# Memory keys and values projected in 512 columns per bank, keys of all four heads normed together

## The chip, the cores and the metric

The kernel runs on one core of one Trainium2 chip. The metric is device time in microseconds (us) for one execution. The five engines are named as in the profile: PE is TensorE's products (PEld its weight loads), DVE is VectorE, ACT is ScalarE, POOL is GpSimd, and SP issues most of the DMAs. Each engine takes its instructions strictly in the order in which the program holds them.

## The reference

One layer of a decoder trunk over 1024 tokens of width 1024. The input `x` is normed and projected; three branches (a sparse attention, a convolution module, and cross-attention into 256 memory tokens) are gated, merged, projected and added to `x`; a feed-forward part follows. The change concerns the keys and values of the cross-attention:

```python
kvm = rms_norm(mem, norm_mem) @ w_mem_kv          # mem (256, 1024), w_mem_kv (1024, 2 * 512)
km, vm = jnp.split(kvm, 2, axis=-1)
km = rms_norm(km.reshape(b, -1, MEM_HEADS, MEM_HEAD_DIM), mem_qk_norm[1])   # 4 heads of 128
vm = vm.reshape(b, -1, MEM_HEADS, MEM_HEAD_DIM)
s_m = jnp.einsum('bshd,bmhd->bhsm', qm, km) * (MEM_HEAD_DIM ** -0.5)
o_m = jnp.einsum('bhsm,bmhd->bshd', jax.nn.softmax(s_m), vm)
gm = jax.nn.sigmoid(g_merge)                      # three merge gates, 3 * 1024 columns of w_in
```

## The kernel before, in words

Every product of two float32 matrices is made of three passes: both operands are split into a rounded part and a remainder, and `mm3` adds high x high, high x low and low x high in one PSUM bank. A split is a cast on ScalarE (`split`, L131) and a subtraction, mostly on VectorE (L132). Weights come in units of 512 KB through a staging tile (`st`, two buffers) and are split into a buffer of 128 x 2 x 1024.

Weight buffers lie in two pools: `wsp` with three (tiles `wsl`) and `wfp` with two (tiles `fsl`). A pool gives its buffers out in the order in which the program asks, so a later tile waits until the tile that held its buffer has been read for the last time. The helper `anyslab` takes from both: its own counter `turn[0]` sends calls 2 and 4 of every five to `wfp`. PSUM has seven banks for general use (`ps`) and one (`pf`) for the merge gates while these run.

The stages in order of time: the rows of `x` are normed (`norm_row`) and turned into XN (`turn_pair`, whose two parts are L227 on ScalarE and L228 on VectorE), with the memory queries' projection (`queries`) between them; the convolution's inputs, whose 124 taps (L466, L467) run on VectorE along the later projections; the branch gates (L489 to L507, weights `wg`); the compression of the block keys and values (`compress`, weights `cmp_w1`); the memory rows, normed and turned into MN; the memory keys KM and values VM; the memory attention, along with the sparse attention's query projection; that attention's keys and values; the sparse attention itself; then the three output projections with the gates, the output product, and the feed-forward part.

Before the change, keys and values are made in four rounds of two weight units each. A round (`tok_proj` over `row_units`) covers 256 columns, two heads, for both token tiles, and puts them side by side in one bank; each product has 256 columns. The keys of two heads are normed (`heads_norm`), scaled (`gain_mul`), transposed and split before the next round begins.

The order on each engine is made by a scheduler. It takes instructions by a priority, which is their place in the program unless the code changes it, and by its own estimate of when each can start. The merge-gate products (L1016 to L1034) are written under `low(FILL)`, which puts them behind everything else: they are taken where the scheduler sees TensorE free. There are 24 of these weight units, each used for two halves of 24 products, 48 groups in all; the first twelve units may run at any time, the others are tied to points spread over the sparse attention. Each unit has a buffer of `wfp`, and each group the single bank `pf`, emptied by ScalarE (L1033). In the texts below these products are called fillers.

Of the kernel before, what the change touches and what calls it, by code (L numbers as in the profile page):

```python
# [17 lines left out]
P = 128  # L18
# [3 lines left out]
KT = D // P  # L22
# [17 lines left out]
def hybrid_layer_kernel(  # L40
# [4 lines left out]
    nc = tc.nc  # L45
    x, mem, out = x[0], mem[0], out[0]
    w_in, w_mem_kv, w_out = w_in[0], w_mem_kv[0], w_out[0]
# [19 lines left out]
    def nm(s):  # L67
        count[0] += 1
        return f"{s}_{count[0]}"
# [16 lines left out]
    def t4(shape, dt=F32):  # L86
        return t4p.tile([P] + shape, dt, tag="t4", name=nm("t4"))

    def t2(shape, dt=F32, p=P):
        return t2p.tile([p] + shape, dt, tag="t2", name=nm("t2"))  # L90
# [8 lines left out]
    def bank(shape, dt=F32, p=P, at=None):  # L99
        if at is None:  # L100
            turn[1] += 1
            at = order[turn[1] % len(order)]
        return psp[at].tile([p] + shape, dt, tag=f"ps{at}", name=nm("ps"))
# [26 lines left out]
    def split(hi, lo, src, eng=None):  # L130
        m = nc.scalar.copy(hi, src)  # L131
        return m, (eng or nc.vector).tensor_tensor(lo, src, hi.bitcast(F32), op=OP.subtract)  # L132
# [12 lines left out]
    def mm(o, a, b, start, stop):  # L145
        m = nc.tensor.matmul(o, a, b, start=start, stop=stop)  # L146
        n = 1
        for d in o.shape[1:]:
            n *= d
        products.append((m.ins, n if a.dtype == F32R else 4 * n))  # L150
        return m

    def mm3(o, ah, al, bh, bl, start, stop):
        first = mm(o, ah, bh, start, False)
        mm(o, ah, bl, False, False)
        mm(o, al, bh, False, stop)
        return first
# [8 lines left out]
    ident = identr.bitcast(F32)  # L166
# [115 lines left out]
    def row_units(w, c0, alloc=wslab, eng=None):  # L282
        return [unit(w[u * 512:(u + 1) * 512, c0:c0 + 256].rearrange("(k p) c -> p k c", p=P), [4, 256], alloc, eng)
                for u in range(2)]
# [7 lines left out]
    def tok_proj(ws, tp, act=xn, alloc=bank, between=None):  # L292
        o = alloc([2, 256])
        for tt in range(2):
            if tt == 1 and between is not None:
                between()
            t = 2 * tp + tt
            half, a = t // 4, (t % 4) * P
            for k in range(KT):
                w = ws[k // 4]  # L300
                mm3(o[:, tt, :], act(0, k, half, a, a + P), act(1, k, half, a, a + P), w[:, 0, k % 4, :],
                    w[:, 1, k % 4, :], k == 0, k == KT - 1)
        return o

    def wide_unit(w, c0, u, alloc=wslab):

        st = stage.tile([P, 2, 512], F32, tag="st", name=nm("st"))
        nc.sync.dma_start(st, wide_rows(w, c0, u))
        if alloc is t4:
            w_ = (t4([2, 512], F32R), t4([2, 512], F32R))  # L310
        else:
            w_ = alloc([2, 2, 512])
            w_ = (w_[:, 0], w_[:, 1])
        split(w_[0], w_[1], st)
        return w_

    def wide_rows(w, c0, u):
        return w[u * 256:(u + 1) * 256, c0:c0 + 512].rearrange("(k p) c -> p k c", p=P)
# [76 lines left out]
    b = bank([2 * KT])  # L395
    nc.tensor.transpose(b, rows, ident[:2 * KT, :2 * KT])
    nc.vector.tensor_copy(gcol, b)
    ws = [wide_unit(w_in, C_QM, u, alloc=slab) for u in range(2)]
# [31 lines left out]
    b = bank([4, TAPS + 3])  # L430
# [5 lines left out]
    b = bank([2, 16])  # L436
# [58 lines left out]
    for half in range(2):  # L495
        c = slice(half * 512, (half + 1) * 512)
        ps = bank([512])
# [6 lines left out]
    b = bank([NT, 24])  # L504
# [78 lines left out]
    def mn(hl, k, half, a, b):  # L583
        return MN[k // 4][:, hl, k % 4, a:b]

    KM = slab([2, 4, 256])
    VM = slab([2, 2, 512])
    for hp in range(2):
        ps = tok_proj(row_units(w_mem_kv, hp * 256), 0, mn).rearrange("p t (h d) -> p t h d", h=2)
        if hp == 0:  # L590
            turn_keys(cat, products[-1][0])
            compress_out(1, hv, products[-1][0])
        kn = t2([2, 2, P])
        heads_norm(ps, kn)
        gain_mul(kn, gm[:, 1, :])
        b = bank([2, 256])
        for h in range(2):
            for tt in range(2):
                nc.tensor.transpose(b[:, h, tt * P:(tt + 1) * P], kn[:, tt, h, :], ident)
        split(KM[:, 0, 2 * hp:2 * hp + 2, :], KM[:, 1, 2 * hp:2 * hp + 2, :], b)  # L600
    for hp in range(2):
        ps = tok_proj(row_units(w_mem_kv, 512 + hp * 256), 0, mn)
        split(VM[:, 0, :, hp * 256:(hp + 1) * 256], VM[:, 1, :, hp * 256:(hp + 1) * 256], ps)

    msc, exps, stored = float(P) ** -0.5, [], []

# [100 lines left out]
    ws = [wide_unit(w_in, C_Q, u, alloc=slab if u == 3 else wslab) for u in range(4)]  # L707
# [13 lines left out]
    ws = [wide_unit(w_in, C_KV, u, alloc=t4 if u == 3 else wslab) for u in range(4)]  # L721
# [9 lines left out]
    for t in range(NT):  # L731
# [5 lines left out]
        kn = t2([2, 2, 64])  # L737
# [278 lines left out]
    with low(FILL):  # L1016
        j, ws = 0, {}
        halves = [(n_, h_) for n_ in range(3 * KT) for h_ in range(2)]
        halves[-4:] = [(n_, h_) for h_ in range(2) for n_ in (3 * KT - 2, 3 * KT - 1)]
        for n_, h_ in halves:  # L1020
# [5 lines left out]
            ps = fbank([512])  # L1026
# [72 lines left out]
    for n_, (br, wt) in enumerate(branches):  # L1099
        ins = nxt  # L1100
        for dp in range(4):
            w = unit(wt[0, :, dp * 256:(dp + 1) * 256].rearrange("(k p) c -> p k c", p=P), [4, 256],
                     alloc=anyslab if n_ else fslab if dp < 2 else wslab,
# [5 lines left out]
            for d_ in (2 * dp, 2 * dp + 1):  # L1109
# [6 lines left out]
                for half in range(2):  # L1116
                    z = zz[:, half * 512:(half + 1) * 512]
                    ps = (anybank if n_ or dp < 2 and half else bank)([512])
# [5 lines left out]
                    a = acc[dp][:, d_ % 2, half * 512:(half + 1) * 512]  # L1124
# [454 lines left out]
```

## Time and profile before

| what | value |
|---|---|
| median of 3 runs | 1663.55 us (1663.47 to 1663.68) |
| profiled execution, first to last instruction | 1663.0 us; the profile gives no other time of its own, and the median lies 0.5 us above |
| TensorE busy | 1630.5 us |
| VectorE, ScalarE, GpSimd busy | 1103.2, 746.5, 669.7 us |
| mean granted clock of TensorE | 0.998 |
| memory keys and values | 216 to 260 us of the span |
| memory attention and sparse attention's projections | up to about 428 us |
| sparse attention | about 428 to 830 us |

Busy time is an average over stages with different limits, and a matmul counts as busy until its modelled end, so that short waits between products do not show as idle. What a wait is worth is read in its own stage: from the timeline, which shows the instructions of an engine in order of time with the idle time before each in brackets and what ended it, and from the busy times by stage.

### The profile page before, as it was taken

The page shows a single profiled execution, that of the slowest core. Times are in us where ns is not written, and L with a number is a line of the kernel's source. Part 1 is how long each engine was busy: PE and PEld are TensorE (multiplying, and loading weights), DVE is VectorE, ACT ScalarE, POOL GpSimd, SP SyncE. Part 2 cuts the span into 40 slices and gives each one's busy share as a digit, 9 for nine tenths or more (in the row PEclk, how much of TensorE's full clock was granted, in tenths as well). Part 3 has the DMA queues.
Part 4 walks back from the last instruction along what each step waited for, and adds up shares of the span by engine and source line. Part 5 has one row for each costly group of instructions (what it writes and reads, how often), then busy time and mean ns, then how long its engine had stood idle before and what let it go on. Part 6 is the DMA issues. An engine that isn't in the chain of part 4 may idle for free.

```text
span 1663.0 us, 22705 instructions
## 1 busy us (share of the span) xinstructions
PE 1630.5 (98%) x7952; PEld 1363.2 (82%) x7952; DVE 1103.2 (66%) x1829; ACT 746.5 (45%) x1371; POOL 669.7 (40%) x564
## 2 busy tenths in 40 slices
PE   7999999999999999999999999999999999999999
PEld 6888898777878888888788888788888888888887
DVE  6489989798666666557586867865445555376655
ACT  6311354442577666666665355533222232243332
POOL 0011003572467767555215431565657767400000
PEclk9999999999999999999999999999999999999999
DMA  8453456664355556447754442233333445893763
GB/s 283 157 182 102 152 152 178 203 192 125 108 143 167 165 163 177 134 133 249 245 193 140 177 126 115 89 116 100 97 125 123 153 156 183 297 391 108 241 216 126
DMA packets 252218, 277.89 MB, mean 167 GB/s; under 512 B 24308, under 2 KB 174116, under 8 KB 250566
## 3 DMA queue, kind: packets, MB, share of 16 engines
q1 hardware_dynamic: 245190, 263.83, 49.3%
q10 hardware_dynamic: 6912, 12.59, 2.0%
q8 instruction: 63, 1.03, 0.3%
q14 instruction: 53, 0.43, 0.1%
HBM read 191.43 MB, written 84.93 MB: 166 GB/s over the span
## 4 chain that ended last, share of the span: by engine, by line
PE 71%; DVE 4%; POOL 2%; issue 2%; ACT 2%; DMA 1%; SPq 0%; DVEq 0%; POOLq 0%; ACTq 0%
PE ps L146 37%; PE pf L146 15%; PE ps L1513 11%; PE ps L1287 4%; PE ps L965 2%; PE pf L1513 1%; DVE slab L467 1%; POOL slab L666 1%; PE pf L1287 1%; POOL t L643 0%; ACT t L637 0%; DMA wd<-wsl 0%; POOL t L132 0%; PE ps L951 0%; DVE t L132 0%
## 5 line engine op out<-in xcount | busy, mean ns | idle before, releaser
L146 PE MATMUL ps<-slab,wsl 128*128 128x512 f32 (+2 forms) x1688 | 362.8, 373 | 0.3 <-ACT slab L131 0.3
L146 PEld LDWEIGHTS ps<-slab,wsl 128*128 128x128 f32 x1688 | 298.2, 188 | 57.4 <-issue 1.2
L146 PE MATMUL pf<-slab,fsl 128*128 128x512 f32 x1236 | 309.5, 394 | 3.6 <-ACT fz L1033 3.3
L146 PEld LDWEIGHTS pf<-slab,fsl 128*128 128x128 f32 x1236 | 226.9, 188 | 49.0 <-ACT fz L1033 5.7
L1409 DVE TENSOR_TENSOR t<-ps,t 128x512 f32<-128x512 f32 x130 | 89.0, 689 | 120.6 <-PE ps L146 119.3
L467 DVE SCALAR_TENSOR_TENSOR slab<-slab,cw 128x1019 f32<-128x1019 f32 (+16 forms) x120 | 166.0, 1387 | 1.4
L146 PE MATMUL ps<-slab,fsl 128*128 128x512 f32 x684 | 164.4, 394 | 2.0 <-DVE slab L132 1.2
L146 PE MATMUL ps<-slab,slab 128*128 128x512 f32 (+1 forms) x628 | 155.1, 381 | 6.9 <-POOL slab L666 4.1
L146 PEld LDWEIGHTS ps<-slab,fsl 128*128 128x128 f32 x684 | 128.7, 189 | 30.4 <-DVE slab L132 1.6
L146 PEld LDWEIGHTS ps<-slab,slab 128*128 128x128 f32 x628 | 113.7, 190 | 31.7 <-POOL slab L666 5.9
L1513 PE MATMUL ps<-wsl 128*128 128x512 f32 x495 | 118.9, 389 | 0.0
L1513 PEld LDWEIGHTS ps<-wsl 128*128 128x128 f32 x495 | 92.9, 188 | 19.3
L132 DVE TENSOR_TENSOR wsl<-st,wsl 128x1024 fp32r<-128x1024 f32 x58 | 83.7, 1445 | 32.6 <-ACT wsl L131 31.7
L131 ACT CAST wsl<-st 128x1024 fp32r<-128x1024 f32 x61 | 64.0, 1050 | 75.7 <-PE ps L146 30.3
L146 PE MATMUL ps<-wsl,slab 128*128 128x512 f32 (+1 forms) x480 | 97.2, 349 | 0.4 <-DVE slab L228 0.3
L146 PE MATMUL ps<-slab,qt 128*128 128x384 f32 (+6 forms) x400 | 93.8, 338 | 0.8 <-DVE sm L841 0.7
L146 PE MATMUL ps<-t,slab 128*128 128x256 f32 (+1 forms) x404 | 88.5, 319 | 1.5 <-DVE t L132 1.1
L146 PEld LDWEIGHTS ps<-wsl,slab 128*128 128x128 f32 x480 | 76.4, 189 | 11.3 <-DVE slab L228 0.5
L1422 POOL TENSOR_TENSOR t<-t,t 128x512 f32<-128x512 f32 x21 | 39.9, 1900 | 112.7 <-DVE t L1409 55.5
L131 ACT CAST wsl<-t 128x1024 fp32r<-128x1024 f32 x43 | 45.3, 1054 | 87.6 <-POOL t L128 28.7
L1513 PE MATMUL ps<-fsl 128*128 128x512 f32 x330 | 80.2, 389 | 0.0
L1130 POOL TENSOR_TENSOR slab<-slab,t 128x512 f32<-128x512 f32 x32 | 47.8, 1515 | 80.3 <-DVE t L1129 80.3
(255 smaller groups left out, 2942.5 us busy)
## 6 DMA issues: line engine op xcount, KB each, us to landing
t<-in_w_down_dram SPq DMA_DIRECT2D x70, 256.0 KB, 3.9
fst<-in_w_in_dram SPq DMA_DIRECT2D x24, 512.0 KB, 4.2
zd<-fz ACTq DMA_DIRECT2D x48, 256.0 KB, 2.4
slab<-wd SPq DMA_DIRECT2D x24, 512.0 KB, 4.6
t<-zd SPq DMA_DIRECT2D x24, 512.0 KB, 3.4
st<-in_w_gate_dram SPq DMA_DIRECT2D x22, 512.0 KB, 3.8
st<-in_w_up_dram SPq DMA_DIRECT2D x22, 512.0 KB, 4.2
ad<-t SPq DMA_DIRECT2D x44, 256.0 KB, 2.3
```

The costliest lines, as they stand in the source:

```text
L131: m = nc.scalar.copy(hi, src)
L132: return m, (eng or nc.vector).tensor_tensor(lo, src, hi.bitcast(F32), op=OP.subtract)
L146: m = nc.tensor.matmul(o, a, b, start=start, stop=stop)
L467: return nc.vector.scalar_tensor_tensor(acc[:, s:], u[:, :S - s], cw[:, ct, 30 - s:31 - s], acc[:, s:], op0=OP.mult, op1=OP.add)
L666: part = nc.gpsimd.tensor_tensor(PT[:, 1, mb], PT[:, 1, mb].bitcast(F32), PT[:, 0, mb].bitcast(F32), op=OP.subtract)
L965: nc.tensor.transpose(b[:, j - j0, h, :], tiles[h][:, j * P:(j + 1) * P], ident)
L1130: nc.gpsimd.tensor_tensor(a, a, z, op=OP.add)
L1287: nc.tensor.matmul(B[j], a_(ha, k, j), w[:, hb, k % 2, :], start=start and k == 0 and n_ == 0, stop=stop and k == 3 and n_ == 2, skip_grou ...
L1409: nc.vector.tensor_tensor(o, a_, b_, op=OP.add)
L1422: nc.gpsimd.tensor_tensor(u4, u4, c22, op=OP.mult)
L1513: nc.tensor.matmul(B[t], a_, b_, start=start and k == 0 and j == 0, stop=k == FH - 1 and j == 2, skip_group_check=True)
```

## The change

The four rounds become two halves. Each half loads four weight units of 256 rows by 512 columns (`wide_unit` instead of `row_units`, with `anyslab` as the allocator), and makes for each of the two token tiles one bank of 512 columns, with products of 512 columns. The keys of a token tile, all four heads, are normed and scaled at once; they are kept, and transposed and split between the value products.

```diff
-    for hp in range(2):
-        ps = tok_proj(row_units(w_mem_kv, hp * 256), 0, mn).rearrange("p t (h d) -> p t h d", h=2)
-        if hp == 0:
+    def mem_proj(ws, tt):
+        o = bank([512])
+        for k in range(KT):
+            hi, lo = ws[k // 2]
+            mm3(o, mn(0, k, 0, tt * P, tt * P + P), mn(1, k, 0, tt * P, tt * P + P), hi[:, k % 2, :], lo[:, k % 2, :],
+                k == 0, k == KT - 1)
+        return o
+
+    ws = [wide_unit(w_mem_kv, 0, u, alloc=anyslab) for u in range(4)]
+    kns = []
+    for tt in range(2):
+        ps = mem_proj(ws, tt).rearrange("p (a h d) -> p a h d", a=1, h=4)
+        if tt == 0:
             turn_keys(cat, products[-1][0])
             compress_out(1, hv, products[-1][0])
-        kn = t2([2, 2, P])
+        kn = t2([1, 4, P])
         heads_norm(ps, kn)
         gain_mul(kn, gm[:, 1, :])
-        b = bank([2, 256])
-        for h in range(2):
-            for tt in range(2):
-                nc.tensor.transpose(b[:, h, tt * P:(tt + 1) * P], kn[:, tt, h, :], ident)
-        split(KM[:, 0, 2 * hp:2 * hp + 2, :], KM[:, 1, 2 * hp:2 * hp + 2, :], b)
-    for hp in range(2):
-        ps = tok_proj(row_units(w_mem_kv, 512 + hp * 256), 0, mn)
-        split(VM[:, 0, :, hp * 256:(hp + 1) * 256], VM[:, 1, :, hp * 256:(hp + 1) * 256], ps)
+        kns.append(kn)
+    ws = [wide_unit(w_mem_kv, 512, u, alloc=anyslab) for u in range(4)]
+    for tt in range(2):
+        ps = mem_proj(ws, tt)
+        b = bank([4, P])
+        for h in range(4):
+            nc.tensor.transpose(b[:, h, :], kns[tt][:, 0, h, :], ident)
+        c = slice(tt * P, (tt + 1) * P)
+        split(KM[:, 0, :, c], KM[:, 1, :, c], b)
+        split(VM[:, 0, tt, :], VM[:, 1, tt, :], ps)
```

Before, all eight units took `wsl` buffers. Now `anyslab` gives five of them `wsl` and three `fsl`, ahead of the fillers' units in the program. Its counter stands eight calls further at every later use (the second and third branch's weights, the last products of the feed-forward part), so that there the two pools alternate from another point on.

The order on the engines changes well before the edited lines. In the following rows, which the engine takes from top to bottom, `ps` and `pf` are PSUM banks, the first name behind the arrow is the streamed operand and the second the stationary one; a number behind the tile tells one tile from the next. First TensorE, between the convolution's last products (`ps_1201`) and the branch gates' (`ps_1252`, whose stationary operand is `wg`). Before:

```order
L146 MATMUL ps_1201<-slab_406,wsl_1117 128x512 x6
L146 MATMUL pf_6652<-slab_403,fsl_6621 128x512 x6
L146 MATMUL pf_6652<-slab_404,fsl_6621 128x512 x6
L146 MATMUL pf_6652<-slab_405,fsl_6621 128x512 x6
L146 MATMUL pf_6652<-slab_406,fsl_6621 128x512 x6
L146 MATMUL ps_1252<-slab_196,t_170_1247 56x512 x4
```

Now:

```order
L146 MATMUL ps_1201<-slab_404,wsl_1117 128x512 x6
L146 MATMUL ps_1201<-slab_405,wsl_1117 128x512 x6
L146 MATMUL ps_1201<-slab_406,wsl_1117 128x512 x6
L146 MATMUL ps_1252<-slab_196,t_170_1247 56x512 x4
L146 MATMUL ps_1252<-slab_197,t_170_1247 56x512 x4
```

The 24 fillers between the two are gone. In the same way the first 24 fillers have left the projections of `x`, and 24 more the compression.

Second, TensorE at the memory keys: `slab_1556` and `slab_1557` are MN, `ps_1606` before and `ps_1616` now the first keys. Before:

```order
L146 MATMUL pf_6685<-slab_198,fsl_6682 128x512 x4
L146 MATMUL pf_6685<-slab_199,fsl_6682 128x512 x6
L146 MATMUL ps_1606<-wsl_1598,slab_1556 128x256 x11
L146 MATMUL pf_6713<-slab_403,fsl_6682 128x512 x6
L146 MATMUL pf_6713<-slab_404,fsl_6682 128x512 x6
L146 MATMUL pf_6713<-slab_405,fsl_6682 128x512 x6
L146 MATMUL pf_6713<-slab_406,fsl_6682 128x512 x2
L146 MATMUL ps_1606<-wsl_1598,slab_1556 128x256
L146 MATMUL ps_1606<-wsl_1603,slab_1557 128x256 x12
```

Now, with the first value products (`ps_1720`) among them:

```order
L236 MATMUL ps_1585<-identr,slab_1481 128x128 x3
L146 MATMUL ps_1616<-wsl_1598,slab_1556 128x512 x6
L146 MATMUL ps_1616<-fsl_1603,slab_1556 128x512 x6
L146 MATMUL ps_1616<-wsl_1608,slab_1557 128x512 x5
L146 MATMUL ps_1720<-wsl_1702,slab_1556 128x512 x6
L146 MATMUL ps_1616<-wsl_1608,slab_1557 128x512
L146 MATMUL ps_1616<-fsl_1613,slab_1557 128x512 x6
```

No filler stands here any more, and the weights come from both pools. The first filler of the new order (`pf_6528`) stands behind 84 of the 96 memory products.

Third, ScalarE just ahead of the memory keys, where L227 makes the parts of MN. Before:

```order
L131 CAST wsl_1687<-st_1685 128x1024
L552 ACTIVATE t_207_1544,sm_1545<-ps_1541 128x64
L227 ACTIVATE slab_1556<-ps_1558,gcol 128x256
L227 ACTIVATE slab_1556<-ps_1567,gcol 128x256
L138 ACT_TABLE_LOAD
L138 ACTIVATE sm_1547<-sm_1545 128x1
L227 ACTIVATE slab_1557<-ps_1576,gcol 128x256
```

Now:

```order
L552 ACTIVATE t_207_1544,sm_1545<-ps_1541 128x64
L138 ACT_TABLE_LOAD
L138 ACTIVATE sm_1547<-sm_1545 128x1
L227 ACTIVATE slab_1556<-ps_1558,gcol 128x256
L131 CAST wsl_1702<-st_1700 128x1024
L227 ACTIVATE slab_1556<-ps_1567,gcol 128x256
L227 ACTIVATE slab_1557<-ps_1576,gcol 128x256
```

The table load has moved ahead of all eight parts, and the cast of a value weight (`wsl_1702`) between the first and the second of them.

## The prediction

> **What bounds the kernel now.** I read the page's busy shares and chain first, then the stages. The page:
>
> ```profile
> PE 1630.5 (98%) x7952; PEld 1363.2 (82%) x7952; DVE 1103.2 (66%) x1829; ACT 746.5 (45%) x1371; POOL 669.7 (40%) x564
> PE 71%; DVE 4%; POOL 2%; issue 2%; ACT 2%; DMA 1%; SPq 0%; DVEq 0%; POOLq 0%; ACTq 0%
> ```
>
> TensorE is busy for 98% of the span and holds most of the chain that ended last. So the time is TensorE's work plus its waits, and I look at what is under that 98%. The busy times by stage (columns: stretch, its length, then busy time and instructions of PE, PEld, DVE, ACT, POOL; clock, DMA share, GB/s):
>
> ```profile
> 28.00:80.00 52.00, 51.60 (x245) 42.29 (x245) 27.02 (x49) 24.13 (x54) 0.00 (x0) 1.00 0.49 163
> 80.00:158.00 78.00, 78.00 (x345) 64.56 (x345) 66.78 (x60) 12.99 (x16) 10.09 (x8) 1.00 0.45 135
> 158.00:165.00 7.00, 6.67 (x30) 5.01 (x30) 6.13 (x9) 1.43 (x3) 1.35 (x2) 1.00 0.86 247
> 165.00:205.00 40.00, 40.00 (x228) 32.69 (x227) 38.40 (x33) 12.06 (x27) 0.00 (x0) 1.00 0.49 166
> 217.00:248.00 31.00, 30.73 (x211) 28.53 (x212) 25.46 (x34) 13.09 (x25) 3.36 (x2) 1.00 0.49 144
> 248.00:428.00 180.00, 171.79 (x863) 142.28 (x863) 153.63 (x220) 74.39 (x180) 79.29 (x71) 1.00 0.55 166
> 428.00:780.00 352.00, 347.58 (x1896) 298.65 (x1894) 216.90 (x751) 234.37 (x576) 226.53 (x242) 1.00 0.53 162
> 780.00:830.00 50.00, 47.32 (x243) 38.22 (x242) 28.85 (x43) 29.41 (x44) 19.16 (x14) 1.00 0.74 235
> ```
>
> From 80 to 205 VectorE is nearly full too. And part of TensorE's work is filler: the merge-gate products, which write the one bank `pf` and run at lowest priority wherever the scheduler sees a hole. The same stages for the tile `pf` alone:
>
> ```profile
> 28.00:80.00 52.00, 6.78 (x24) 4.51 (x24) 0.00 (x0) 0.59 (x1) 1.00 0.49 163
> 158.00:165.00 7.00, 5.60 (x24) 4.50 (x24) 0.00 (x0) 0.58 (x1) 1.00 0.86 247
> 205.00:217.00 12.00, 6.00 (x24) 4.36 (x24) 0.00 (x0) 0.00 (x0) 1.00 0.48 157
> 217.00:248.00 31.00, 11.68 (x48) 8.80 (x48) 0.00 (x0) 1.79 (x3) 1.00 0.49 144
> 248.00:428.00 180.00, 52.54 (x216) 39.74 (x216) 0.00 (x0) 4.71 (x8) 1.00 0.55 166
> ```
>
> 72 fillers run before 217 us and 48 in the memory projection (217 to 248). They hide waits; this is what the change touches.
>
> **The change part by part.** *The products.* 192 products of 256 columns become 96 of 512, on the same data. Their prices, from groups and stretches without waits:
>
> ```profile
> L146 PE MATMUL ps<-wsl,slab 128*128 128x256 f32 x192 | 25.4, 285 | 0.3 <-DVE slab L228 0.3
> 223.25 4.59 PE L146 MATMUL ps<-wsl,slab 128*128 128x256 f32 x37
> 79.72 78.72 PE L146 MATMUL ps<-slab,wsl 128*128 128x512 f32 x346
> ```
>
> 78.72/346 = 0.2275 us for 512 columns, so 96 cost 21.8. The 192 cost 25.4 by the group, and 192 x 4.59/37 = 23.8 by the dense stretch. The saving lies between 2.0 and 3.6; I take 3.0. [...]
>
> Norms, gains, splits and transposes handle the same elements in as many instructions; the keys' transposes move behind the value products, and the first memory score waits for the last of their splits:
>
> ```profile
> 236.69 0.68 DVE L382 TENSOR_TENSOR t<-ps,sm 128x512 f32<-128x512 f32 x1
> 248.44 1.60 PE L146 MATMUL ps<-slab,t 128*128 128x256 f32 x12
> ```
>
> I cost them at nothing: the 48 value products and 44 fillers (20.9 us) run meanwhile, and VectorE has 31 - 25.46 = 5.5 us free in that stage. Without that cover the norms, gains and splits of one half, four such steps of 0.68 us, would be 2.7 us. The weights move the same bytes in as many loads.
>
> *The filler's buffers.* Of the eight weight units, three now take buffers of `wfp` (two buffers), which only fillers used until then. In program order they stand ahead of the fillers, so the first filler's weights wait until the memory products have read theirs. The changed order shows it: up to the first memory score it has 44 fillers instead of 120, and none before the memory products. 76 x 0.2275 = 17.3 us of filler go later. What matters is whether each hole stays open without them:
>
> ```profile
> 32.75 1.26 DVE L228 SCALAR_TENSOR_TENSOR slab<-ps,gcol,slab 128x256 fp32r<-128x256 f32 x3
> 36.60 0.75 DVE L217 TENSOR_SCALAR slab<-slab,sm 128x1024 f32<-128x1024 f32 x1
> 39.62 0.60 PE L236 MATMUL ps<-identr,slab 128*128 128x128 f32 x4
> ```
>
> Hole A (28 to 40, 24 fillers, 5.5 us). The real products there need the parts that are ready at 32.75 + 1.26 = 34.01, the next transposes the rows normed at 37.35; TensorE came to them at 39.62. Most of the filler time was in the way and comes back. 0.5 to 2.5 us stay open; I take 1.5.
>
> ```profile
> 158.28 5.60 PE L146 MATMUL pf<-slab,fsl 128*128 128x512 f32 x24
> 164.22 7.54 PE L146 MATMUL ps<-slab,t 128*56 128x512 f32 x32 [0.33 <-DVE t L132]
> 152.23 5.99 DVE L467 SCALAR_TENSOR_TENSOR slab<-slab,cw 128x1022 f32<-128x1022 f32 x5
> 162.85 0.48 DVE L492 MEMSET t<- 128x512 f32 x1
> 163.81 0.36 DVE L132 TENSOR_TENSOR t<-st,t 128x192 fp32r<-128x192 f32 x1 [0.47 <-ACT t L131]
> ```
>
> Hole B (158 to 164). The gate products wait for `wg`, zeroed and split on VectorE, behind its taps of the convolution; even after 24 fillers they still waited 0.33. VectorE's order there is unchanged, so the hole moves with the stage and stays: 5.5 us (5.0 to 5.9).
>
> ```profile
> 205.16 3.43 PE L146 MATMUL pf<-slab,fsl 128*128 128x512 f32 x14
> 208.43 3.73 PE L146 MATMUL ps<-slab,wsl 128*128 128x128 f32 x32
> 198.29 0.38 SPq L534 DMA_DIRECT2D wsl<-in_cmp_w_dram  x1
> DMA to landing us min/median/max: 6.4/7.3/8.2
> ```
>
> Hole C (205 to 208, 14 fillers, 3.2 us). The 32 products behind it need the last quarter of `cmp_w1`, issued at 198.29; with 6.4 to 8.2 us to landing (two such loads) it is there between 204.7 and 206.5. TensorE, free at 205.16, would wait 0 to 1.3 us; I take 0.7, and the rest of the 3.2 comes back.
>
> ```profile
> 214.07 2.57 PE L146 MATMUL pf<-slab,fsl 128*128 128x512 f32 x10
> 216.47 1.05 PE L146 MATMUL ps<-wsl,slab 128*128 128x256 f32 x5
> 217.78 0.97 PE L146 MATMUL ps<-wsl,slab 128*128 128x256 f32 x6 [0.26 <-DVE slab L228]
> 218.59 4.82 PE L146 MATMUL pf<-slab,fsl 128*128 128x512 f32 x20
> 218.36 1.26 DVE L228 SCALAR_TENSOR_TENSOR slab<-ps,gcol,slab 128x256 fp32r<-128x256 f32 x3
> ```
>
> Hole D (214 to 223). The memory products wait for the normed memory rows, whose parts ScalarE (L227) and VectorE (L228) make; these end at 219.62. From 214.07 to 217.78 five products (0.65) were possible, so about 3.1 us were a wait; of the 20 fillers after it only some 0.4 us. In the changed order on ScalarE a weight's cast (about 1 us) stands among these parts, and the parts come behind a table load. 2 to 6 us stay open; I take 3.5.
>
> Together the holes leave 1.5 + 5.5 + 0.7 + 3.5 = 11.2 us open (7.5 to 15.7).
>
> *The clock.* Two stretches later in the run, each one step of the granted clock long:
>
> ```profile
> 1048.85:1052.26 3.41, 1.66 (x7) 0.92 (x6) 3.41 (x7) 2.77 (x6) 0.00 (x0) 1.00 0.47 139
> 1052.26:1055.67 3.41, 3.41 (x10) 2.66 (x9) 3.41 (x5) 0.78 (x1) 0.00 (x0) 0.50 0.00 0
> ```
>
> After 3.41 us in which TensorE worked 1.66, the clock was 0.50 for the next 3.41, which costs 1.7 us of work. B is long enough for it wherever the steps fall, D probably: 2 x 1.7 = 3.4 (1.7 to 3.4). [...]
>
> *The deferred fillers.* Their 17.3 us are done later, and shorten the time only where TensorE idles then. Counted in the two orders, the changed one is 76 fillers behind at the first memory score, 48 at the first scores of the sparse attention, 24 near that attention's end, level after it. So 28 (6.4 us) go into the stage 248 to 428, which idles 180 - 171.79 = 8.2 us; 24 (5.5 us) into 428 to 780, which idles 4.4; 24 into the tail, which idles 2.7. At most 6.4 + 4.4 + 2.7 = 13.5 us find idle time; fillers come in pieces of 0.23 us and an idle stretch is seldom where the scheduler saw it, so at least 3. I take 8.
>
> **Sum.** The deferred work itself is neutral (it left the front), so: -3.0 (products) + 11.2 (holes) + 3.4 (clock) - 8.0 (idle time filled) = +3.6 us. The profiled span is 1663.0 and the median of the runs shown 1663.55; I put the change on the latter: **1667.2 us**. All terms at their low ends give -3.6 + 7.5 + 1.7 - 13.5 = -7.9, at their high ends -2.0 + 15.7 + 3.4 - 3.0 = +14.1.
>
> **The rivals.**
>
> *The later stages swallow the fillers* (faster). The place is 248 to 428, where VectorE is busy for 153.63 of 180 and TensorE waits for it and for GpSimd's parts; up to 13.5 us of fillers vanish there and behind it. With the clock paid once, D at its low end of 2 and the products at their best: -3.6 + 9.7 + 1.7 - 13.5 = -5.7, so 1658. It decides from 11.6 us of idle time filled on (8.0 + 3.6). For it: the three stages idle for 15.3 together. Against it: fillers were there before as well (216 in 248 to 428) and left this idle time.
>
> *VectorE's lead gives the time back* (no change). Hole A closes 4 us earlier, and VectorE, full from 80 to 205, starts its taps earlier by that; if it carries the lead into the memory attention, that stage, with VectorE busy for 85%, gets shorter by about 4: +3.6 - 4 = 0, so 1663. Against it: the taps are tied to the products' order, and TensorE fills that stage to 95%.
>
> *The holes stay and nothing is filled* (slower). The attention is TensorE's own stage (347.58 of 352), the 48 fillers that reach it cost their full 10.9 us and only 3 go into idle time before: -3.0 + 11.2 + 3.4 - 3.0 = +8.6, so 1672; with D at 6, 1675.
>
> *The products are not cheaper* (the change doesn't do what it says). The last value weights need a buffer that the key products free, so the 512-column stream may break: 0 instead of -3.0, and 1670. For it: all eight units are now needed by the first token tile of each half, not four.
>
> **How the numbers follow.** The forecast has 0.40, its own range 1664 to 1670. The rivals: fillers swallowed 0.15, VectorE's lead 0.22, nothing filled 0.15, products not cheaper 0.08. What a measurement of this kernel can tell from no change is about 0.2%, 3.3 us: the bounds are 1660.2 and 1666.9. Slower: the forecast's part above 1666.9 (a good half, 0.23), and the last two (0.23): 0.46. Faster: the first rival, 0.15. The rest, 0.39, is no change that can be told. The range that leaves 2 in 10 out goes to the swallowed fillers below and the open holes above: 1658 to 1676.
>
> **What would show it.** Right: no `pf` product before the memory products; TensorE idle for about 5 us ahead of the gate products (L500), released by VectorE's split; a granted clock of 0.5 right after; 96 products of 128x512 at L593 costing about 22 us; the first memory score near 248; more `pf` in 248 to 428 than 216. Wrong: if the gate products start without a long wait, hole B was the fillers' own making; if the stage 428 to 830 is no longer than 402 us, the fillers were swallowed; if the first memory score comes before 240, the front was not held by VectorE; if the down products at the end run slower, the other choice of weight buffers there, which I cost at nothing since TensorE has no idle time in them, is to blame.

## The result, and the profile after

The changed kernel takes 1682.72 us (median of 4 runs, 1679.98 to 1685.23) against 1663.62 us: a ratio of 1.0109 with a 95% interval of 1.0095 to 1.0123. In a second set beside the experiments it took 1681.23 us (1679.64 to 1682.47). So it is 17 to 19 us slower. The direction was right; the size was not: the time lies above the range, and above the sum of all the prediction's terms at their high ends (1663.55 + 14.1 = 1677.7). The profiled execution is the fastest of the first four: 1679.98 us, with a span of 1678.3.

The page of the changed kernel, busy shares and chain:

```profile
PE 1634.2 (97%) x7856; PEld 1361.8 (81%) x7856; DVE 1102.5 (66%) x1829; ACT 748.9 (45%) x1371; POOL 666.3 (40%) x564
PE 74%; DVE 2%; ACT 1%; issue 1%; DMA 1%; POOL 1%; SPq 0%; ACTq 0%; DVEq 0%
```

There are 96 products fewer, and TensorE is yet busy for 3.7 us longer: where its clock was at half, the same products count as busy for longer, as the 32 gate products below show (9.34 us against 7.54). VectorE, ScalarE and GpSimd are as they were, within 3.4 us. The holes, in the timeline of TensorE:

```profile
30.00 0.73 PE L146 MATMUL ps<-slab,slab 128*128 128x512 f32 x2 [1.05 <-ACT slab L227]
31.33 4.62 PE L146 MATMUL ps<-slab,slab 128*128 128x512 f32 x19 [0.60 <-DVE slab L228]
37.18 0.66 PE L236 MATMUL ps<-identr,slab 128*128 128x128 f32 x4 [1.23 <-DVE slab L217]
...
161.65 9.34 PE L146 MATMUL ps<-slab,t 128*56 128x512 f32 x32 [5.53 <-DVE t L132]
...
205.83 3.81 PE L146 MATMUL ps<-slab,wsl 128*128 128x128 f32 x32 [1.21 <-DMA wsl<-in_cmp_w_dram]
...
211.47 1.53 PE L236 MATMUL ps<-identr,slab 128*128 128x128 f32 x12 [1.00 <-DVE slab L217]
214.53 1.01 PE L146 MATMUL ps<-wsl,slab 128*128 128x512 f32 x3 [1.52 <-ACT slab L227]
216.93 1.22 PE L146 MATMUL ps<-wsl,slab 128*128 128x512 f32 x2 [1.39 <-ACT slab L227]
218.66 0.79 PE L146 MATMUL ps<-wsl,slab 128*128 128x512 f32 x1 [0.51 <-DVE slab L228]
```

The numbers in brackets are the waits: A 1.05 + 0.60 + 1.23 = 2.9 us, B 5.53, C 1.21, D 1.00 + 1.52 + 1.39 + 0.51 = 4.4. No filler stands among these rows. The 32 gate products behind B take 9.34 us; before they took 7.54. The granted clock says why (columns as in the prediction's table by stage; the clock is the third number from the end):

```profile
155.00:171.00 16.00, 10.47 (x38) 5.70 (x38) 12.94 (x14) 1.98 (x3) 1.27 (x2) 0.79 0.71 214
211.00:226.00 15.00, 11.10 (x39) 8.11 (x40) 12.07 (x19) 7.23 (x17) 0.00 (x0) 0.77 0.45 139
254.00:438.00 184.00, 175.63 (x854) 145.62 (x852) 145.10 (x214) 72.50 (x177) 78.11 (x72) 0.98 0.51 157
438.00:800.00 362.00, 359.52 (x1961) 309.64 (x1960) 220.74 (x762) 240.28 (x583) 227.24 (x243) 1.00 0.53 161
800.00:843.00 43.00, 40.84 (x210) 33.45 (x209) 21.57 (x27) 24.11 (x35) 16.46 (x12) 1.00 0.72 246
```

The clock was at half for 6.8 us from 158.7, for 6.8 us from 216.8, and for 3.4 us each from 343.1 and 377.2. The fillers alone (`pf`), in the same table:

```profile
226.00:254.00 28.00, 11.02 (x44) 8.11 (x44) 0.00 (x0) 0.59 (x1) 1.00 0.63 183
254.00:438.00 184.00, 60.85 (x244) 45.98 (x244) 0.00 (x0) 5.89 (x10) 0.98 0.51 157
```

44 fillers instead of 120 run ahead of the memory attention, and 244 instead of 216 in it, as the order showed.

Where the time went, stage by stage. "Work" is the products of a stage, each at the spacing from start to start that products of its size have in the kernel before (the lower quartile of it). Products that started while the clock was at half are counted once more, which is the column "clock" (in the changed kernel's trace products of 512 columns start 0.43 us apart there, and 0.23 elsewhere). What is then left of the stage's length is waiting. All are differences, after less before, in us:

| up to | length | fillers | work | clock | waiting |
|---|---|---|---|---|---|
| first memory score (253.8 us, was 248.4) | +5.4 | -76 | -14.0 | +5.4 | +13.9 |
| first scores of the sparse attention (437.9, was 428.2) | +4.3 | +28 | +2.3 | +3.9 | -1.9 |
| output projections (843.1, was 827.2) | +6.2 | +48 | +11.0 | 0 | -4.8 |
| end | -0.8 | 0 | -0.2 | -1.8 | +1.3 |
| sum | +15.1 | 0 | -1.0 | +7.5 | +8.6 |

The work ahead of the first memory score fell by less than its 76 fillers (17.2 us), since more of the other products now stand ahead of it (3.2 us, after what the change saves). By the same count the second set's profiled execution (*e0* below; 17.4 us longer than before) has work -1.0, clock +9.7 and waiting +8.5: what it is longer than this one comes from the clock.

### The profile page after: what moved, and what is told of

Its sections match the earlier page's. It is cut to its first block, busy times and chain, and to the rows that moved or that the text cites. A ratio compares the mean times of both kernels' runs of the same rounds, so it can differ in the third digit from the quotient of the medians.

```text
span 1678.3 us, 22491 instructions
## 1 busy us (share of the span) xinstructions
PE 1634.2 (97%) x7856; PEld 1361.8 (81%) x7856; DVE 1102.5 (66%) x1829; ACT 748.9 (45%) x1371; POOL 666.3 (40%) x564
## 4 chain that ended last, share of the span: by engine, by line
PE 74%; DVE 2%; ACT 1%; issue 1%; DMA 1%; POOL 1%; SPq 0%; ACTq 0%; DVEq 0%
PE ps L146 38%; PE pf L146 17%; PE ps L1525 11%; PE ps L1299 4%; PE ps L977 2%; PE pf L1525 1%; PE pf L1299 1%; PE ps L963 0%; DMA slab<-ud 0%; PE ps L236 0%; POOL slab L678 0%; DVE wsl L132 0%; DVE t L128 0%; ACT slab L131 0%; ACT fz L1045 0%
## 5 line engine op out<-in xcount | busy, mean ns | idle before, releaser
L146 PE MATMUL pf<-slab,fsl 128*128 128x512 f32 x1236 | 314.6, 396 | 3.7 <-ACT fz L1045 3.5
L146 PE MATMUL ps<-wsl,slab 128*128 128x512 f32 x348 | 89.0, 401 | 3.4 <-ACT slab L227 2.9
L131 ACT CAST wsl<-st 128x1024 fp32r<-128x1024 f32 x60 | 62.9, 1050 | 62.1 <-PE ps L146 18.6
L132 DVE TENSOR_TENSOR t<-ps,t 128x512 fp32r<-128x512 f32 (+2 forms) x96 | 61.0, 640 | 39.4 <-ACT t L131 38.7
L131 ACT CAST wsl<-t 128x1024 fp32r<-128x1024 f32 x41 | 43.1, 1054 | 93.0 <-POOL t L128 37.1
```

## The experiments

**Who takes the fillers' buffers.** *e1* leaves `wfp` to the fillers; the fourth unit of each half goes into a slab:

```diff
-    ws = [wide_unit(w_mem_kv, 0, u, alloc=anyslab) for u in range(4)]
+    ws = [wide_unit(w_mem_kv, 0, u, alloc=slab if u == 3 else wslab) for u in range(4)]
...
-    ws = [wide_unit(w_mem_kv, 512, u, alloc=anyslab) for u in range(4)]
+    ws = [wide_unit(w_mem_kv, 512, u, alloc=slab if u == 3 else wslab) for u in range(4)]
```

> The changed kernel, with the memory weights kept out of the fillers' pool: three units of each half in wsl, the fourth in a slab. In the order on TensorE 48 fillers again stand ahead of the gate products and 120 ahead of the memory attention, as before the change. Theory (the loss comes from the fillers' buffers): the holes A to D are filled, the clock stays up, only the cheaper products remain: 1663.6 - 3.0 = 1660.6 us (1659 to 1664). Rival (the 512-column order itself is slow: keys of all heads at once, transposes behind the value products): the loss stays, 1676 to 1683. Second rival (the shifted turn of the two pools in the later stages, which this kernel also undoes): 1660 as well, to be told from the theory by the kernel that shifts the turn alone.

Measured: 1671.21 us (1670.04 to 1673.22), ratio 1.0043 (1.0028 to 1.0058). All three expectations missed, and the time lies between them: 10 to 11.5 us of the loss go with the buffers, but 6.5 stay, where the theory left none. Up to the memory keys the trace is that of before (hole B filled, the first step at half clock at 511 us), so the loss that stays has to come from behind them.

*e2* is the counterpart, the kernel before with the new allocation alone:

```diff
-        ps = tok_proj(row_units(w_mem_kv, hp * 256), 0, mn)
+        ps = tok_proj(row_units(w_mem_kv, hp * 256, alloc=anyslab), 0, mn)
...
-        ps = tok_proj(row_units(w_mem_kv, 512 + hp * 256), 0, mn)
+        ps = tok_proj(row_units(w_mem_kv, 512 + hp * 256, alloc=anyslab), 0, mn)
```

> The kernel before, with its eight memory units of 256 columns given out by anyslab, so that three of them take buffers of wfp; products, norms and transposes as before the change. In the order no filler stands ahead of the gate products. Theory (fillers' buffers): the whole loss without the saving of the products: 1682.7 + 3.0 = 1686 us (1680 to 1688). Rival (the 512-column order): no loss, 1664.

Measured: 1689.39 us (1688.49 to 1694.17), ratio 1.0159 (1.0137 to 1.0180), above the theory's range as well. The buffers alone cost more than the whole change. The rival falls for this part: the old order pays without any product of 512 columns in the memory keys and values. The gate products behind hole B, in e1 and in e2:

```profile
163.51 7.55 PE L146 MATMUL ps<-slab,t 128*56 128x512 f32 x32 [0.38 <-DVE t L132]
...
159.91 10.00 PE L146 MATMUL ps<-slab,t 128*56 128x512 f32 x32 [5.56 <-DVE t L132]
```

*e3* moves the counter of the two pools and nothing else:

```diff
     KM = slab([2, 4, 256])
+    turn[0] += 8
```

> The kernel before, with the counter of the two pools moved on by eight ahead of the memory keys and nothing else changed, so that the later uses of both pools alternate as in the changed kernel. Theory: 1663.6 us, no change that can be told (1662 to 1666). Rival (the later stages' weights wait in their new turn): up to the whole loss, 1670 to 1683.

Measured: 1664.17 us (10 runs, 1663.17 to 1666.36), ratio 1.0000 (0.9990 to 1.0009). In the order of before, the later stages' other choice of buffers is free, as predicted.

**The weight units outermost.** *e4* makes both token tiles' banks at once:

```diff
...
+        for u in range(4):
+            hi, lo = wide_unit(w_mem_kv, c0, u)
+            for tt in range(2):
+                for k in (2 * u, 2 * u + 1):
+                    mm3(os_[tt], mn(0, k, 0, tt * P, tt * P + P), mn(1, k, 0, tt * P, tt * P + P), hi[:, k % 2, :],
+                        lo[:, k % 2, :], k == 0, k == KT - 1)
...
```

> The changed products of 512 columns, but with the weight units as the outer loop: each unit serves both token tiles in two banks at once and is free after 12 products, so three wsl buffers are enough and no buffer of wfp is taken. Fillers ahead of the gate products: 48, as before. Theory: 1663.6 - 3.0 = 1660.6 us (1658 to 1664), perhaps the better form of the change. Rival (the keys of all heads at once come late for the memory attention, both token tiles ending together): 3 to 6 us more than that, 1664 to 1667.

Measured: 1670.74 us (1668.94 to 1671.36), ratio 1.0038 (1.0023 to 1.0052): the rival, and dearer than it said (1664 to 1667). It and e1 point to the keys of all heads being late, which is tested further down: in e4 both token tiles' keys end together, and the first memory score comes at 260.7 us, 12.3 later than before.

**Hole B by itself.** *e5* is the kernel before with an order for its fillers (`gate0` is the first gate product):

```diff
...
                 first = mm3(ps, w[:, 0, k, :], w[:, 1, k, :], xn(0, k, h_), xn(1, k, h_), k == 0, k == KT - 1)
+                if k == 0 and 0 < 2 * n_ + h_ < 2 * N_EARLY:
+                    follow(first, products[gate0][0], "fillers behind the gates")
```

> The kernel before, with its fillers from the second group of 24 on tied behind the first gate product (an order alone: the same products, later). So the first hole keeps its fillers, hole B has none, and every later filler stands 24 products further back. No change in the memory stage. Theory, with the sizes that the changed kernel's trace showed: 5.5 us of idle time, two steps at half clock (3.4 us), less the part of 24 deferred fillers that later idle time takes (about a third, 1.9 us): 1664.6 + 7.0 = 1671.6 us (1669 to 1674). By the prediction's sizes (one step, 1.7 us, and 8.0/17.3 of the deferred work hidden, 2.5 us): 1669.3. Rival (the wait for the gates' weights is the fillers' own doing): 1664.6.

Measured: 1671.13 us (1670.21 to 1673.07), ratio 1.0043 (1.0030 to 1.0056), 7.0 us over the 1664.17 of the kernel before beside it. That is the size corrected by the changed kernel's trace, not the prediction's. TensorE's timeline and the two steps of the clock:

```profile
163.48 9.70 PE L146 MATMUL ps<-slab,t 128*56 128x512 f32 x32 [6.04 <-DVE t L132]
...
161.30:164.71 3.41, 1.23 (x3) 0.68 (x4) 2.80 (x5) 0.35 (x1) 0.07 (x2) 0.51 0.86 236
164.71:168.13 3.42, 3.42 (x9) 1.68 (x8) 3.35 (x3) 0.00 (x0) 0.00 (x0) 0.50 1.06 346
```

So the wait is VectorE's, and not the fillers' own doing. And one hole of 6 us drew two steps at half clock: the first step began while TensorE still waited and had it busy for 1.23 of its 3.41 us, and the next was at half too.

**What the half clock costs, and what filling a hole brings.** *e6* is the changed kernel with idle products in hole B:

```diff
+    last = products[-1][0]
+    with low(FILL):
+        junk = fbank([512])
+        for j in range(24):
+            m = mm(junk, xn(0, 0, 0)[:, 0:P], xn(0, 1 + j % 7, 0), j == 0, j == 23)
+            if j == 0:
+                follow(m, last, "idle products behind the convolution's")
     gT = t4([S])
```

> The changed kernel, with 24 products of 512 columns put into hole B whose result nobody uses (lowest priority, tied behind the convolution's last product, operands that are ready). They take the idle time and nothing else: the gate products still wait for VectorE and all fillers still come later. Theory (the halved clock behind the hole is a cost of its own): the clock stays full at the gate products and the time falls by 3.4 us against the changed kernel of the same call (2 to 5). Rival (the clock's halves fall where TensorE waits anyway, and cost nothing): no change, within 1 us; if the products delay the gates, slower by up to 1 us.

*e0* is the changed kernel again:

> The changed kernel once more, as the level for the two kernels derived from it: 1682.7 us (1680 to 1685).

Measured: e0 1681.23 us (ratio 1.0099, 1.0084 to 1.0115), e6 1683.02 us (1680.49 to 1685.56; ratio 1.0112, 1.0098 to 1.0126). The gain is not there in the whole time. In its place it is (e6, then e0, TensorE's timelines):

```profile
161.58 7.55 PE L146 MATMUL ps<-slab,t 128*56 128x512 f32 x32 [1.64 <-DVE t L132]
168.97 4.95 PE L146 MATMUL ps<-slab,wsl 128*128 128x512 f32 x21
```

```profile
161.41 8.95 PE L146 MATMUL ps<-slab,t 128*56 128x512 f32 x32 [5.54 <-DVE t L132]
170.20 4.93 PE L146 MATMUL ps<-slab,wsl 128*128 128x512 f32 x21
```

The gate products start at the same time and are 1.4 us shorter. Later in e6's execution there are other steps at half clock: two from 366.3, behind 3.4 us in which TensorE was busy for 1.20, one at 407.3, and two from 823.7, behind 3.4 us with 1.60, where e0 has one each at 342.0 and 376.1. So the local price of a step is shown, 1.4 us here; that taking one step away shortens the run is not. Nor does the mean granted clock alone tell the time: one of e6's four runs has 0.946, the others 0.992 to 0.994, and at 1681.26 us it is not the longest. Why stays open.

**What the deferred fillers cost where they now stand.** *e7*:

```diff
-            for k in range(KT):
+            ks = KT if 2 * n_ + h_ > 3 else 2
+            for k in range(ks):
...
```

> The changed kernel with 72 merge-gate products left out (the first four groups sum 2 of their 8 blocks of the width, so those gate columns are not the layer's), which are 16.4 us of TensorE's work, about what the change deferred. It prices the deferred work where it now stands. If the later idle time swallows the share that the prediction gave it (8.0 of 17.3), the time falls by 8.8 us against the changed kernel; by the share that the changed kernel's trace shows (6.0 of 17.3), by 10.7; if nothing is swallowed, by 14 to 16.4.

Measured: 1664.13 us (11 runs, 1661.68 to 1666.38), 17.1 us under e0. By the whole time nothing of the deferred work is swallowed, and the two smaller sizes look wrong. The two profiled executions say otherwise (worked out as in the table above, against e0): work -16.3, waiting +5.7, clock -4.9 us, together -15.5 of the spans' -15.7. By them 5.7 of 16.3 us had been in idle time, much the share of 6.0 of 17.3, and fewer steps at half clock make up for it. But 3.4 of the 4.9 us are two steps in e0, at 14.3 and 31.4 us, where the two programs are still the same. And e7's profiled execution is its longest, with a granted clock of 0.995 where the median of its runs has 0.993, near e0's 0.990 to 0.995. So the clock doesn't explain the 17.1 us of the medians, and how much of the deferred work idle time hides stays open, between nothing (medians) and about a third (traces).

**What is left without the buffers: the keys.** *e8* keeps the keys of before and widens the values alone, in e4's loop:

```diff
-    for hp in range(2):
-        ps = tok_proj(row_units(w_mem_kv, 512 + hp * 256), 0, mn)
-        split(VM[:, 0, :, hp * 256:(hp + 1) * 256], VM[:, 1, :, hp * 256:(hp + 1) * 256], ps)
+    vs = [bank([512]) for _ in range(2)]
+    for u in range(4):
+        hi, lo = wide_unit(w_mem_kv, 512, u)
...
+    for tt in range(2):
+        split(VM[:, 0, tt, :], VM[:, 1, tt, :], vs[tt])
```

*e9* does the opposite, from e1:

```diff
-    for tt in range(2):
-        ps = mem_proj(ws, tt)
+    for hp in range(2):
+        ps = tok_proj(row_units(w_mem_kv, 512 + hp * 256), 0, mn)
...
-        split(VM[:, 0, tt, :], VM[:, 1, tt, :], ps)
+        split(VM[:, 0, :, hp * 256:(hp + 1) * 256], VM[:, 1, :, hp * 256:(hp + 1) * 256], ps)
```

*e10* is e1 with the keys turned (transposed) right behind their norm:

```diff
         gain_mul(kn, gm[:, 1, :])
         kns.append(kn)
+        b = bank([4, P])
+        for h in range(4):
+            nc.tensor.transpose(b[:, h, :], kns[tt][:, 0, h, :], ident)
+        c = slice(tt * P, (tt + 1) * P)
+        split(KM[:, 0, :, c], KM[:, 1, :, c], b)
```

(with the same lines gone from the loop over the values).

> The keys of the kernel before (two rounds of 256 columns, each normed and turned at once), and the values alone in 512 columns, the weight units as the outer loop, three wsl buffers, no buffer of wfp. Theory (with the fillers' buffers left alone, what is left of the loss comes from keys that are turned late): half of the products' saving and no loss, 1663.8 us (1662 to 1665.5). Rival (512 columns in themselves, or the four units that a half needs at once): as the kernel with both halves wide and no wfp, 1670 to 1672.

> The counterpart: keys of all four heads at once, in 512 columns, turned between the value products, as in the change; values in two rounds of 256 columns as before; no buffer of wfp. Theory (late keys): the first row maximum of the memory attention stays near 259 us instead of 250, and the time near 1671 (1669 to 1673). Rival (the values' form): 1664.

> The change with the fillers' buffers left alone (1671.2 us), and each token tile's keys turned and split right behind their norm instead of between the value products; all products still 512 columns. Theory (late keys): the first row maximum of the memory attention comes back from 259 to about 252 us, and most of the loss with it: 1666 us (1662 to 1668). Rival (the norm of all heads at once is late by itself, whatever the place of the turning): 1671.

Measured: e8 1664.77 us (11 runs, 1662.73 to 1668.40; ratio 1.0006, 0.9997 to 1.0015), e9 1674.59 us (1670.83 to 1675.56; 1.0059, 1.0047 to 1.0072), e10 1668.04 us (11 runs, 1664.76 to 1672.11; 1.0023, 1.0014 to 1.0032). With the old keys nothing that can be told is lost, with the wide keys as much as in e1 and more (above the theory's range, but far from the rival); turning them at once brings back half of e1's loss, less than the theory's 1666. The first row maximum of the memory attention on VectorE (kernel before, e8, e10, e1, e9):

```profile
250.02 0.68 DVE L632 TENSOR_REDUCE sm<-ps 128x2 f32<-128x512 f32 x1
```

```profile
251.19 1.29 DVE L638 TENSOR_REDUCE sm<-ps 128x2 f32<-128x512 f32 x2
```

```profile
256.98 0.68 DVE L644 TENSOR_REDUCE sm<-ps 128x2 f32<-128x512 f32 x1
```

```profile
259.42 1.28 DVE L644 TENSOR_REDUCE sm<-ps 128x2 f32<-128x512 f32 x2
```

```profile
261.32 1.28 DVE L643 TENSOR_REDUCE sm<-ps 128x2 f32<-128x512 f32 x2
```

Against the kernel before, with e4 beside them (waiting and clock by each trace, as in the table above; all in us):

| kernel | first row maximum later by | time over before | waiting | clock |
|---|---|---|---|---|
| e8, old keys | 1.2 | 0.5 | -0.1 | +1.6 |
| e10, turned at once | 7.0 | 3.8 | +2.4 | +3.5 |
| e1, no `wfp` | 9.4 | 6.6 | +5.8 | +1.0 |
| e9, wide keys alone | 11.3 | 10.3 | +7.1 | +3.3 |
| e4, units outermost | 12.2 | 6.1 | -0.3 | +5.5 |

In the first four, the later the memory attention's chain of row maxima begins, the longer the run, by 0.4 to 0.9 us for each of them. e4 falls out of this order: its chain begins last and its loss is not the largest, and in its trace the loss is in the clock and not in waiting. So wide keys are shown to cost 4 to 10 us by themselves, and their lateness goes with it; that the start of the row maxima is the whole cause is not shown. The turning is not all of it: e10, turned at once, still begins 7 us late. Which step of the wide keys makes the rest was not followed further. Nor was the slab that e1, e9 and e10 take for every fourth unit tried alone; e4 takes none and loses as much as e1.

**Late keys inside the change.** *e11* is the changed kernel, buffers and all, with e10's lines:

> The changed kernel as it is, with its weights from both pools, but each token tile's keys turned and split right behind their norm. With the fillers' buffers left alone that step was worth 3.2 us (1671.2 to 1668.0), with the first row maximum 2.4 us earlier. If the late keys are a loss of their own beside the fillers', the changed kernel's 1682 us falls by about 3, to 1679 (1677 to 1680.5). If they are covered there (the fillers that come late are work that TensorE can do while it waits for the row maxima), nothing changes: 1682 (1680.5 to 1685). Slower than 1685 would say that the buffers alone cost more than the change does, as they did in the old order (1689.4).

Measured: 1689.66 us (1687.24 to 1690.03; ratio 1.0152, 1.0138 to 1.0166). The third case: turning the keys at once makes the changed kernel 7 to 8 us slower, and brings it to the time of e2, the old order with the same buffers. By the trace the two go on alike: 24 fillers ahead of the memory attention in both, then 192 up to the sparse attention's keys, and 864 in its scores. In the changed kernel 44 stand ahead: while TensorE waits for the late keys, it does 20 fillers more. But that is 4.6 us of 17.3 deferred; most of the difference arises behind the sparse attention. From its last score to the first product of the output projections the changed kernel takes 44.5 us (e0 too), e2 52.1 and e11 50.0. In both TensorE waits there where the changed kernel's does not, longest 1.5 us for ScalarE (L131). Both also have two steps at half clock between 1049 and 1081 us, where the changed kernel's first profile has none and e0 one. Why the tail differs, with nearly the same work in it, stays open, and so does why the buffers cost 25 us alone (e2) but 10 to 11.5 beside the wide keys (e1).

## Why the prediction was wrong, by its steps

The step of the prediction that failed most is the term of the clock: it was sized at one step at half clock for each of two holes, 3.4 us, and the trace has 7.5. Smaller misses, all to the same side, are in the idle time filled, the holes, and the products' price.

- **The mechanism was right.** Units in `wfp`, no filler in the front, holes open, fillers late: e1 and e2 show it from both sides. No `pf` product stands before the memory products, TensorE is idle for 5.53 us ahead of the gate products, released by VectorE's split, and the clock is at half behind it. The sign that missed is the first memory score, at 253.8 and not near 248.
- **Hole B**: 5.5 predicted, 5.53 in the changed kernel and 6.04 in e5. **C**: 0.7 (0 to 1.3), measured 1.21. **D**: 3.5 (2 to 6), measured 4.4. **A**: 1.5 (0.5 to 2.5), measured 2.9, over its upper bound: I took the parts' ends from the kernel before, and left out that the first parts, from L227, are waited for too (1.05). Sum of the four 14.0 by their rows, 13.9 by the table, 11.2 predicted.
- **The clock** is the term that failed most: 2 x 1.7 = 3.4 with an upper bound of 3.4, against 9.3 at four places, less the one step of before that went, 7.5. The price of a step was right (1.4 to 2.0 us, and 0.5 for the first of hole B, where TensorE still waited). The count was wrong: I allowed one step for each of two holes. Each drew two, and two more fell in the memory attention, at waits for GpSimd's splits (L678; 1.00 and 1.34 us ahead of the one, 1.03 and 1.80 ahead of the other) that the prediction doesn't name. Two steps are not certain: of the twelve holes B and D that the traces of this case leave open, ten drew two steps and two drew one (B in e0, D in e2). In e0 and e11 hole A drew one as well, at 31.4 and 32.8 us, where the prediction allowed none.
- **The deferred fillers**: 8.0 us hidden (3 to 13.5). Waiting fell by 1.9 + 4.8 = 6.7 us behind the first memory score, and rose by 1.3 at the end; the profiled execution of e7 gives much the same share, the median of e7's runs gives none. By the trace the term is in its range and 1.3 too high. The sign "no longer than 402 us" came out on the forecast's side: the stage from 428 to 830 now runs from 437.9 to 843.1, 405.2 (399.0 before). But I compared work with idle time and forgot that what stays idle there can be followed by a step: the one at 343.1 stands behind 3.41 us in which TensorE was busy for 1.48.
- **The products**: 3.0 saved (2.0 to 3.6). By their spacing the saving is 1.0: 192 at 0.118 us against 96 at 0.226. And e8, with half of it, is not faster than before. My prices for 256 columns were read from rows that end with the last product's whole duration, 0.28 us: in the stretch of 37 products (4.59 us) they start 0.120 us apart, so that 192 cost 23.0 and not 23.8, and the group's 25.4 has such an end at every break of the stream.
- **The keys' transposes, at nothing**: wrong for the wide keys without the buffers, and not to be seen in the change. Without the buffers' loss, wide keys cost 6.5 us (e1), of which the place of the turning is 3.2 (e1 to e10). I had named the stage's cover, 20.9 us of products and fillers on TensorE. That covers TensorE; the chain of row maxima on VectorE begins 9.4 us later all the same. Inside the change, the late keys are even the better form (e11).
- **The pools' turn in the later stages, at nothing**: right, in the order of before (e3).

In the trace: 2.7 (holes) + 4.1 (clock) + 1.4 and 1.3 (idle time, behind the first score and at the end) + 2.0 (products) = 11.5 us over the +3.6 predicted, which gives +15.1. The medians differ by 17 to 19, and the profiled execution is the shortest of its set; the changed kernel's eight runs have a mean granted clock of 0.990 to 0.995, against 0.997 to 0.999 in the runs of the kernel before beside the second four. Of the rivals "nothing is filled" came closest (1672), though the trace has more filled than its 3 us, and fell short by the same clock. "The later stages swallow the fillers" and "VectorE's lead" did not come: the first memory score is 5.4 us later, not earlier. "The products are not cheaper" holds in part, but not by its mechanism: behind hole D the memory products have no wait. What the prediction says for it is a misreading too: a half has four units, where a round had two, so that its first token tile needs four and not eight.

No version here beats the kernel before. e8 is the change's best part, and cannot be told from it.

## What to carry to other kernels

A pool's buffers go out in program order: before a tensor is given a buffer of another pool, look at who else lives there and where in the program its first use stands, since low-priority work that hides waits may be held back hundreds of microseconds ahead of the edited lines. When filler work leaves a hole, look at the clock too: holes of 4 to 6 us like B and D mostly drew two steps here (ten of twelve), and 1.93 and 2.83 us of waiting within 3.41 us downstream drew one each. And cover must be named for the chain that goes on behind a moved step, not only for the engine on which the step runs.

## What the runs showed of the hardware

In the profiled execution of the change the steps at half clock begin at 15.4, 158.7, 216.8, 343.1 and 377.2 us, which are 42, 17, 37 and 10 times 3.413 us apart; in that of the kernel before at 14.61 and 1052.26, 304 times 3.413 us. So in each of these traces they lie on one grid. From one execution to the next it lies elsewhere against the kernel's work: in e0's, of the same kernel as the first, there are steps at 14.3, 31.4, 342.0 and 376.1, and the three that have a like one in the first begin 1.1 us earlier. Taking all windows of that length behind the first 8 us in the 14 traces, and TensorE's busy share in each:

| busy share of a window | windows | next one at half clock |
|---|---|---|
| under 0.44 | 33 | 33 |
| 0.44 to 0.55 | 34 | 21 |
| 0.55 to 0.60 | 26 | 9 |
| 0.60 to 0.70 | 66 | 2 |
| over 0.70 | some 6600 | 5 |

All seven in the last two lines are windows which were at half clock themselves, where the same work counts for longer (products of 512 columns 0.43 us apart, not 0.23); the changed kernel's is the one from 216.76, busy for 2.73 of 3.41 us at a clock of 0.50. So 1.93 and 2.83 us of waiting within one window were followed by a step in the changed kernel; 1.76 in the kernel before were not, nor were the last wait of hole A (1.23) and hole C's (1.21), each in a window busy for 2.2 of 3.41 us. The changed kernel's windows ahead of its steps at 343.1 and 377.2, and the one of the kernel before:

```profile
339.69:343.10 3.41, 1.48 (x8) 1.04 (x9) 2.21 (x2) 1.07 (x2) 3.41 (x3) 0.99 0.38 114
373.83:377.24 3.41, 0.58 (x4) 0.24 (x2) 2.19 (x3) 0.33 (x1) 3.41 (x3) 0.99 0.56 153
```

```profile
379.80:383.20 3.40, 1.64 (x10) 1.53 (x11) 3.40 (x5) 0.27 (x1) 2.84 (x2) 1.00 0.47 140
```

That the changed kernel's first four runs spread over 5.3 us, and 13 of the kernel before over 4.0, fits a grid that falls differently each time. So do the runs' mean granted clocks: over 81 runs of the changed kernel and the experiments (without the one at 0.946), each against the mean of its own set, 0.001 less of clock goes with 0.8 us more of time (correlation -0.65; e7's runs show no such link). That the grid is the cause was not tried.
